# A hybrid decoder block: how far ahead the ada weights are fetched, how convolutions and SiLUs are spread over the half units, and the precision of the gate sums

## The chip, the core and the metric

One core of one Trainium2 chip runs the whole kernel. The metric is the device time of one execution in microseconds (us); the median of three runs of the kernel before is 1493.07 us (1491.11 to 1493.28).

## The reference

Only one layer and one sequence of 512 tokens are computed, with a model width of 2048.

```
shift, scale, gate = split(silu(c) @ w_ada + b_ada, 3)            # w_ada: 2048 x 6144
h = rms_norm(x) * (1 + scale) + shift                              # 512 x 2048
q_a k_a v_a z_a b_a a_a  q_b k_b v_b z_b  gl_a gl_b = h @ w_in     # w_in: 2048 x 10768
q,k,v = silu(causal_conv4(q_a k_a v_a)); q,k L2-normed
o_a = rms_norm(gated_delta_rule(q, k, v, g, beta)) * silu(z_a)     # 8 heads of 128
o_b = sliding_window_attention(q_b, k_b, v_b) * silu(z_b)          # 16 heads of 64
y = sigmoid(gl_a) * (o_a @ w_branch_gdn) + sigmoid(gl_b) * (o_b @ w_branch_swa)
out = x + gate * (y @ w_out)
```

## The kernel before

Every large product is done in fp32r with both factors split into a high and a low part: three matmuls of 128x128 by 512 stand for one in full precision. A weight **unit** is 512 KB of a weight matrix, loaded by one DMA on SyncE's queue (SP) into one of three `wraw` buffers (`w_dma`, L220); it serves two **half units**. For each half unit ScalarE (ACT) rounds its half of the unit to `whi` (L232), VectorE (DVE) subtracts to get `wlo` (L237), four buffers each, and TensorE (PE) does 12 matmuls. There are 464 half units; here they are H0 to H463, and the units U0, U1, ... (U19 serves H38 and H39, U20 serves H40 and H41).

`run(n)` (L242) writes the program one half unit at a time, in this order: the unit DMAs that are due (U(j+3) is due at H(2j+1)); the casts of the half unit two ahead (so H38's casts are written at H36); one step of each of the `lanes`; then the 12 matmuls. The schedule is by hand: every engine, and SP's queue too, executes its own instructions in the order in which the program wrote them, and waits at an instruction until its semaphores allow it. A tile's buffer is given to the next tile of its tag when all instructions that use the first tile are done, also those written later.

The first lane is `consumer` (L266). It empties three lists: all of `rel` (work that frees PSUM), one item of `hot`, and one item of `cons`. A convolution is two items (`conv_steps`, L409): `a` is a scaled copy and two taps on DVE, `b` is the third tap, a tanh on ACT, and a product on DVE that needs that tanh (L428). `silu2` (L432) is a tanh and such a product. The convolutions of the first group of heads go to `cons` (30 items, from H50), those of the second to `hot` (four items after every eight half units, from H72).

The second lane, `start_lane` (L1404), works out shift and scale while the matmuls already run. h is made in six stages (`STAGES`, 2, 2, 2, 2, 4 and 4 of the 16 column blocks of 128); the matmuls of one stage (`plan_start`) run while `ada_group(g)` prepares the next. Shift and scale of a stage are sums over 16 rows of blocks of `w_ada`: the first `DVEROWS[g]` rows on DVE (L348, L350), the rest on PE (L358, `ps_row`). Their weights come in 64 **pieces** of 512 KB, P0 to P63 (two DMAs each of 256 KB up to P31, L313; one from P32 on, L309), eight for each of the first four stages and sixteen for each of the last two. `ada_dma` sends them in order on SP's queue too; `send(r)`, after row r, sets how far they have been sent: `used` is the number of pieces used by then. Where a piece is put is in `HOMES`: a digit is one of the large buffers that later hold h, `s` a slot of a pool of 22. In the last stage (g = 5, P48 to P63, one row each, rows 0 to 11 on DVE) P60 and P61 have the buffer in which P52 and P53 (rows 4 and 5) were, and P62 and P63 that of P54 and P55 (rows 6 and 7). Its rows are prepared during H32 to H47: rows 0 and 1 at H32, 2 and 3 at H33, 4 and 5 at H35, 6 and 7 at H36. The `send` that reaches P61 is written after row 5, at H35, that which reaches P63 after row 7, at H36; U19 is due at H33, U20 at H35, U21 at H37.

Later lanes hold the delta rule (`gdn_all`, which starts when `cons` is empty), the keys, the attention, and `gate_all` (L1272): for each of four column blocks of 512 DVE sums 16 rows into `ga`, and one fp32 matmul with a matrix of ones adds the partitions (L1301).

Of the kernel before, what the change touches and what calls it, by code (L numbers as in the profile page):

```python
# [16 lines left out]
P = 128  # L17
# [20 lines left out]
def tile_hybrid_block(  # L38
# [32 lines left out]
    def s2(name, dt=F32):  # L71
        return sp.tile([P, 512], dt, tag="s2", name=nm(name), bufs=NS2)
# [7 lines left out]
    def side(name):  # L80
        return pq.tile([P, 512], F32, tag="side", name=nm(name))
# [103 lines left out]
    def split(hi, lo, src):  # L185
        S.copy(hi, src)
        V.tensor_tensor(lo, src, hi.bitcast(F32), op=ALU.subtract)
# [73 lines left out]
                after()  # L261
    run.s = 0

    cons, rel, hot = [], [], []

    def consumer():  # L266

        while True:
            while rel:
                rel.pop(0)()  # L270
            if hot:
                hot.pop(0)()
            if cons:
                cons.pop(0)()
            yield

# [54 lines left out]
    def ada_group(g):  # L331

        k0, nk = STAGES[g]
        nb = nk // 2
        first = [p_[0] for p_ in pieces].index(g)

        def send(r):

            used = first + r * nk // 4
            ada_dma(max(min(used + 12, 60), used + 8) - nada[0])  # L340

        nv = DVEROWS[g]
        av = None
        for r in range(nv):
            w = wada.pop((g, r))
            if r == 0:
                av = s4("accv")[:, 0:512 * nb]
                V.tensor_scalar(av, w, ccol[:, r:r + 1], None, op0=ALU.mult)  # L348
            else:
                V.scalar_tensor_tensor(av, w, ccol[:, r:r + 1], av, op0=ALU.mult, op1=ALU.add)  # L350
            if r % 2:
                send(r + 1)
                yield
        rows_ = [side("ps_row") for _ in range(nb)]
        for r0 in range(nv, 16, 4):
            for b_ in range(nb):
                for j in range(4):
                    TE.matmul(rows_[b_][32 * j:32 * j + 32], lhsT=cpad[:, r0 + j],  # L358
                              rhs=wada[g, r0 + j][:, b_ * 512:b_ * 512 + 512], start=(r0 == nv), stop=(r0 == 12))
            for r in range(r0, r0 + 4):  # L360
                del wada[g, r]
            send(r0 + 4)
            yield
        sums = s4("asum")[:, 0:512 * nb] if av is None else av
        for b_ in range(nb):
            bs = slice(b_ * 512, b_ * 512 + 512)
            if av is None:
                S.copy(sums[:, bs], rows_[b_])
            else:
                V.tensor_tensor(sums[:, bs], rows_[b_], av[:, bs], op=ALU.add)  # L370
        yield
        psum = small("psum", 8)
        for b_ in range(nb):
            ps = side("ps_mod")
            for i in range(4):
                TE.transpose(ps[:, i * P:(i + 1) * P], sums[:, (4 * b_ + i) * P:(4 * b_ + i + 1) * P], ident)
            if av is None:
                pv_ = ps.rearrange("p (i j z) -> p i j z", i=4, j=4)[:, :, :, 0]
            else:
                pv_ = v3(ps, 4)  # L380
            V.tensor_reduce(psum[:, 4 * b_:4 * b_ + 4], pv_, axis=AX.X, op=ALU.add)
        ks = slice(k0, k0 + nk)
        V.tensor_tensor(AB[:, :, ks], v3(psum[:, 0:2 * nk], 2),
                        cols[:, 0, 32:64].rearrange("p (w k) -> p w k", w=2)[:, :, ks], op=ALU.add)
        V.scalar_tensor_tensor(AB[:, 1, ks], AB[:, 1, ks], 1.0, gains[:, ks], op0=ALU.add, op1=ALU.mult)
        yield
        q, r0 = divmod(k0, 4)
        if r0 == 0:
            hhi[q] = hslot(q, 0, "hhi", F32R)
            hlo[q] = hslot(q, 1, "hlo", F32R)  # L390
        for i in range(nk):
            k, r = k0 + i, r0 + i
            a_, b_ = AB[:, 1, k:k + 1], AB[:, 0, k:k + 1]
            src = xnT[k // 2][:, k % 2]
            hf = s2("hf")
            S.activation(hhi[q][:, r], src, AF.Identity, scale=a_, bias=b_)
            if g < 2:
                V.tensor_scalar(hf, src, a_, b_, op0=ALU.mult, op1=ALU.add)
            else:
                S.activation(hf, src, AF.Identity, scale=a_, bias=b_)  # L400
            V.tensor_tensor(hlo[q][:, r], hf, hhi[q][:, r].bitcast(F32), op=ALU.subtract)
            if i % 2:
                yield


    def th_tile():
        return tp.tile([P, T], F32, tag="th", name=nm("th"), bufs=2)

    def conv_steps(o, src, ct):  # L409

        st = {}

        def tap(s):
            wcol = (3 - s) * 24 + ct
            V.scalar_tensor_tensor(st["o"][:, s:], src[:, :T - s], cw[:, wcol:wcol + 1], st["o"][:, s:],
                                   op0=ALU.mult, op1=ALU.add)

        def a():
            st["o"] = o()
            S.activation(st["o"], src, AF.Copy, scale=cw[:, 3 * 24 + ct:3 * 24 + ct + 1])  # L420
            tap(1)
            tap(2)

        def b():
            tap(3)
            th = th_tile()
            S.activation(th, st["o"], AF.Tanh, scale=0.5)
            V.scalar_tensor_tensor(st["o"], th, 1.0, st["o"], op0=ALU.add, op1=ALU.mult)  # L428

        return [a, b]  # L430

    def silu2(o, src):  # L432
        th = th_tile()
        S.activation(th, src, AF.Tanh, scale=0.5)
        V.scalar_tensor_tensor(o, th, 1.0, src, op0=ALU.add, op1=ALU.mult)

    zd = dp.tile([4, P, 1024], F32, name="zd")
    oad = dp.tile([8, P, 1024], F32, name="oad")
# [62 lines left out]
    def plan_tok(w, col, tile_of, consume, last=False):  # L501

        st = {}

        def mm(k):
            def f(hi, lo):
                if not st:
                    while hot:
                        hot.pop(0)()
                    st["ac"] = [acc("acct") for _ in range(NT)]  # L510
                st[k] = hi[:, 0], lo[:, 0]
                if last and k == KT - 2:
                    return
                for t in range(NT):
                    tsl = slice(t * P, (t + 1) * P)
                    for k_ in (k - 1, k) if last and k == KT - 1 else (k,):
                        wh, wl = st[k_]
                        sh, sl = (z[:, tsl] for z in tile_of(k_))
                        TE.matmul(st["ac"][t], lhsT=sh, rhs=wh, start=(k_ == 0), stop=False)  # L519
                        TE.matmul(st["ac"][t], lhsT=sh, rhs=wl, start=False, stop=False)  # L520
                        TE.matmul(st["ac"][t], lhsT=sl, rhs=wh, start=False, stop=(k_ == KT - 1))  # L521
                    if k == KT - 1:
                        consume(t, st["ac"][t])
            return f

        for ku in range(8):
            u = unit(w[ku * 256:(ku + 1) * 256, col:col + 512], 2)
            for hf in range(2):
                half(u, by_rows(2, hf), mm(2 * ku + hf))
# [62 lines left out]
    beta, hbeta, gg, eG, ekd, egl = (gv[:, i] for i in range(6))  # L592
    t0, t1, t2, t3 = (gv[:, 6 + i] for i in range(4))
    alr = kp.tile([P, P], F32R, name="alr")

    def hc(t):
        return t.rearrange("p (h c) -> p h c", h=GH)
# [3 lines left out]
    def gates_prep():  # L601


        nw = KT * 32
        wab = wab_.pop()
        wabr = s4("wabr", F32R)
        S.copy(wabr[:, nw:nw + 96], wab[:, KT * 16:KT * 16 + 96])
        wab3, wabr3 = v3(wab[:, 0:KT * 16], KT), v3(wabr[:, 0:nw], KT)
        S.copy(wabr3[:, :, 0:16], wab3)
        V.tensor_tensor(wabr3[:, :, 16:32], wab3, wabr3[:, :, 0:16].bitcast(F32), op=ALU.subtract)  # L610
        S.copy(alr, alow)
        S.activation(rows[:, 0:8], rows[:, 0:8], AF.Exp)
        wabs.append(wabr)

# [656 lines left out]
    def gate_all():  # L1271
        for ch in range(4):  # L1272
# [24 lines left out]
                yield  # L1297
            V.tensor_tensor(ga[0:1], ga[0:1], bg, op=ALU.add)
            yield
            pg = side("ps_gate")  # L1300
            TE.matmul(pg, lhsT=ones, rhs=ga, start=True, stop=True)  # L1301
            gates[ch] = s2("gb")
            S.activation(gates[ch], pg, AF.Copy, scale=0.5)
            yield
# [124 lines left out]

    def gdn_all():  # L1430
        yield from gdn_gates()
        while cons:
            yield
        yield from gdn_group(g0)
        while run.s < n_g1 + 5:
            yield
        yield from swa_bias()
        yield from gdn_group(g1)
        while run.s < n_swa + 2 or cons:
            yield  # L1440
        yield from swa_attend()
        yield from load_branches()
# [16 lines left out]
            if next(l_, l_) is l_:  # L1459
                lanes.remove(l_)  # L1460
    run(len(halves) - run.s)
    while rel or hot or cons:
        (rel or hot or cons).pop(0)()


_INS = ["x", "c", "w_ada", "b_ada", "norm_gain", "w_in", "conv_w", "a_log", "dt_bias", "gdn_norm_gain",
# [43 lines left out]
```

## Time and profile before

| | |
|---|---|
| median of 3 runs | 1493.07 us (1491.11 to 1493.28) |
| the profiled execution | 1491.63 us, span 1489.9 us |
| PE (matmul) busy | 1456.0 us, 98% |
| DVE, ACT, POOL busy | 846.3, 568.3, 63.8 us |
| granted PE clock over the span | 0.999 |
| DMA | 223.16 MB, mean 150 GB/s; 320 and 357 GB/s in the first two slices of 37.2 us |
| chain that ended last | PE 92%, DMA 3%, DVE 3%, ACT 1%, issue 1% |

A row of the timeline gives start and length in us, engine, line, operation, what it writes and reads, how many were merged, and in brackets the engine's idle time before it with what ended that. SPq is SP's queue: its rows are the issues of DMAs, and a merged row lasts from the first issue to the end of the last. Matmuls overlap: one takes some 390 ns, and the next starts 227 ns after it. Idle time of PE is therefore more than the bracket by the 0.16 us of overlap that is missing.

### The profile page before, as it was taken

What the parts mean: (1) busy time and instruction counts of PE and PEld (TensorE: products, weight loads), DVE (VectorE), ACT (ScalarE), POOL (GpSimd) and SP (SyncE); (2) the same over time, 40 slices, a digit from 0 to 9 for tenths busy, and PEclk for the clock granted to TensorE, in tenths of its full rate; (3) what the DMA queues carried; (4) which work ended last, traced back from release to release, by engine and by line L of the source; (5) the groups of instructions that cost most, each with busy time, mean ns of one, the idle gap of its engine ahead of it and who ended that gap; (6) DMA issues with size and microseconds to landing.
All of it is one profiled execution on the core that took longest, in us unless ns stands there. A gap on an engine that the chain in (4) does not pass through costs nothing.

```text
span 1489.9 us, 19141 instructions
## 1 busy us (share of the span) xinstructions
PE 1456.0 (98%) x7030; PEld 1190.8 (80%) x7030; DVE 846.3 (57%) x1724; ACT 568.3 (38%) x1275; POOL 63.8 (4%) x109
## 2 busy tenths in 40 slices
PE   4999999999999999999999999999999999999998
PEld 2676788788888888888888888888888888888887
DVE  4675977866755435643553578863324766664332
ACT  4424244363333453322442467763332322222221
POOL 0000000120200030200000000000000000000000
PEclk9999999999999999999999999999999999999999
DMA  9988433223522553422433332245547566564432
GB/s 320 357 277 285 146 101 100 84 86 85 156 63 66 170 171 102 143 82 85 134 93 99 102 97 86 86 135 178 169 127 253 193 225 234 183 207 147 156 125 87
DMA packets 163815, 223.16 MB, mean 150 GB/s; under 512 B 14741, under 2 KB 115414, under 8 KB 163722
## 3 DMA queue, kind: packets, MB, share of 16 engines
q1 hardware_dynamic: 155224, 207.87, 44.1%
q0 software_dynamic: 3616, 13.13, 2.6%
q10 hardware_dynamic: 4882, 0.94, 0.3%
q8 instruction: 55, 0.90, 0.2%
q14 instruction: 38, 0.31, 0.1%
HBM read 201.97 MB, written 23.09 MB: 151 GB/s over the span
## 4 chain that ended last, share of the span: by engine, by line
PE 92%; DMA 3%; DVE 3%; ACT 1%; issue 1%; SPq 0%; ACTq 0%
PE acc L190 17%; PE acc L192 17%; PE acc L191 17%; PE acct L520 7%; PE acct L519 7%; PE acct L521 7%; PE acc L553 3%; PE acc L554 3%; PE acc L559 3%; PE ps_row L358 1%; DMA wraw<-in_w_in_dram 1%; PE ps_kk L743 1%; PE ps_pT L1108 1%; PE ps_pv L1124 1%; DMA wada<-in_w_ada_dram 1%
## 5 line engine op out<-in xcount | busy, mean ns | idle before, releaser
L237 DVE TENSOR_TENSOR wlo<-wraw,whi 128x512 fp32r<-128x512 f32 x464 | 320.7, 693 | 446.4 <-ACT whi L232 439.8
L232 ACT CAST whi<-wraw 128x512 fp32r<-128x512 f32 x464 | 286.6, 621 | 585.7 <-PE acc L191 286.9
L190 PE MATMUL acc<-hhi,whi 128*128 128x512 f32 x896 | 356.3, 398 | 1.7 <-ACT whi L232 1.7
L192 PE MATMUL acc<-hhi,wlo 128*128 128x512 f32 x896 | 350.0, 391 | 0.7 <-DVE wlo L237 0.5
L191 PE MATMUL acc<-hlo,whi 128*128 128x512 f32 x896 | 349.2, 390 | 0.0
L192 PEld LDWEIGHTS acc<-hhi,wlo 128*128 128x128 f32 x896 | 168.2, 188 | 37.9 <-DVE wlo L237 1.9
L190 PEld LDWEIGHTS acc<-hhi,whi 128*128 128x128 f32 x896 | 168.4, 188 | 35.8 <-ACT whi L232 2.6
L191 PEld LDWEIGHTS acc<-hlo,whi 128*128 128x128 f32 x896 | 168.5, 188 | 33.0
L553 PE MATMUL acc<-hhi,whi 128*128 128x512 f32 x256 | 102.2, 399 | 4.5 <-ACT part L570 3.5
L190 PE MATMUL acc<-oh,whi 128*128 128x512 f32 x256 | 100.8, 394 | 0.0
L519 PE MATMUL acct<-whi,mh 128*128 128x512 f32 x256 | 100.1, 391 | 0.1
L554 PE MATMUL acc<-hhi,wlo 128*128 128x512 f32 x256 | 99.9, 390 | 0.0
L192 PE MATMUL acc<-oh,wlo 128*128 128x512 f32 x256 | 99.6, 389 | 0.0
L191 PE MATMUL acc<-ol,whi 128*128 128x512 f32 x256 | 99.6, 389 | 0.0
L520 PE MATMUL acct<-wlo,mh 128*128 128x512 f32 x256 | 99.6, 389 | 0.0
L521 PE MATMUL acct<-whi,ml 128*128 128x512 f32 x256 | 99.6, 389 | 0.0
L519 PE MATMUL acct<-whi,hhi 128*128 128x512 f32 x192 | 76.0, 396 | 0.0
L520 PE MATMUL acct<-wlo,hhi 128*128 128x512 f32 x192 | 74.9, 390 | 0.0
L521 PE MATMUL acct<-whi,hlo 128*128 128x512 f32 x192 | 74.8, 390 | 0.0
L559 PE MATMUL acc<-hlo,whi 128*128 128x512 f32 x256 | 68.5, 389 | 0.0
L553 PEld LDWEIGHTS acc<-hhi,whi 128*128 128x128 f32 x256 | 48.0, 188 | 25.6 <-issue 5.1
L572 DVE TENSOR_TENSOR part<-acc,part 128x512 f32<-128x512 f32 x80 | 51.4, 684 | 24.4 <-PE acc L559 24.4
(281 smaller groups left out, 1816.9 us busy)
## 6 DMA issues: line engine op xcount, KB each, us to landing
wraw<-in_w_in_dram SPq DMA_DIRECT2D x168, 512.0 KB, 3.7
wada<-in_w_ada_dram SPq DMA_DIRECT2D x64, 256.0 KB, 6.7
wada<-in_w_ada_dram SPq DMA_DIRECT2D x32, 512.0 KB, 6.3
wgate<-in_w_ada_dram SPq DMA_DIRECT2D x32, 512.0 KB, 5.7
wraw<-in_w_out_dram SPq DMA_DIRECT2D x32, 512.0 KB, 4.1
tgd<-tg SPq DMA_DIRECT2D x16, 512.0 KB, 2.9
wraw<-in_w_branch_gdn_dram SPq DMA_DIRECT2D x16, 512.0 KB, 3.4
wraw<-in_w_branch_swa_dram SPq DMA_DIRECT2D x16, 512.0 KB, 3.8
```

The costliest lines, as they stand in the source:

```text
L190: TE.matmul(o, lhsT=whi, rhs=mhi, start=start, stop=False)
L191: TE.matmul(o, lhsT=whi, rhs=mlo, start=False, stop=False)
L192: TE.matmul(o, lhsT=wlo, rhs=mhi, start=False, stop=stop)
L232: S.copy(casts[s][0], src)
L237: V.tensor_tensor(lo, view(raws[u]), hi.bitcast(F32), op=ALU.subtract)
L519: TE.matmul(st["ac"][t], lhsT=sh, rhs=wh, start=(k_ == 0), stop=False)
L520: TE.matmul(st["ac"][t], lhsT=sh, rhs=wl, start=False, stop=False)
L521: TE.matmul(st["ac"][t], lhsT=sl, rhs=wh, start=False, stop=(k_ == KT - 1))
L553: TE.matmul(st[ci][m], lhsT=hi[:, i, ms], rhs=mh_, start=(k == k0), stop=False)
L554: TE.matmul(st[ci][m], lhsT=lo[:, i, ms], rhs=mh_, start=False, stop=False)
L559: TE.matmul(st[ci][m], lhsT=hi[:, i, ms], rhs=ml_, start=False, stop=(k == k0 + nk - 1))
L572: V.tensor_tensor(part[ci][:, m], st[ci][m], part[ci][:, m], op=ALU.add)
```

## The change

Four things are changed. How far `send` goes ahead of `used`: it was 12 pieces, but no further than P59 until eight ahead is more than that; now it is 8 for the first two stages and wherever `used` is over 52, 10 for the third stage, 12 otherwise. The last product of a SiLU goes to a list `fin` that the consumer empties at the next half unit. The consumer takes an item of `cons` only if `hot` is empty. The sum `ga` is split into a high and a low part in fp32r, and two fp32r matmuls take the place of the fp32 one.

```diff
-    cons, rel, hot = [], [], []
+    cons, rel, hot, fin = [], [], [], []
     def consumer():
         while True:
             while rel:
                 rel.pop(0)()
+            while fin:
+                fin.pop(0)()
             if hot:
                 hot.pop(0)()
-            if cons:
+            elif cons:
                 cons.pop(0)()
             yield
...
         def send(r):
             used = first + r * nk // 4
-            ada_dma(max(min(used + 12, 60), used + 8) - nada[0])
+            ahead = 8 if g < 2 or used > 52 else 10 if g == 2 else 12
+            ada_dma(used + ahead - nada[0])
...
         def b():
             tap(3)
-            th = th_tile()
-            S.activation(th, st["o"], AF.Tanh, scale=0.5)
-            V.scalar_tensor_tensor(st["o"], th, 1.0, st["o"], op0=ALU.add, op1=ALU.mult)
+            silu2(st["o"], st["o"])
...
     def silu2(o, src):
         th = th_tile()
         S.activation(th, src, AF.Tanh, scale=0.5)
-        V.scalar_tensor_tensor(o, th, 1.0, src, op0=ALU.add, op1=ALU.mult)
+        fin.append(lambda: V.scalar_tensor_tensor(o, th, 1.0, src, op0=ALU.add, op1=ALU.mult))
...
                 if not st:
-                    while hot:
-                        hot.pop(0)()
+                    while fin or hot:
+                        (fin or hot).pop(0)()
...
+    onesr = kp.tile([P, P], F32R, name="onesr")
...
+        S.copy(onesr, ones)
...
+            gh_, gl_ = s2("gah", F32R), s2("gal", F32R)
+            split(gh_, gl_, ga)
+            yield
             pg = side("ps_gate")
-            TE.matmul(pg, lhsT=ones, rhs=ga, start=True, stop=True)
+            TE.matmul(pg, lhsT=onesr, rhs=gh_, start=True, stop=False)
+            TE.matmul(pg, lhsT=onesr, rhs=gl_, start=False, stop=True)
...
-        while cons:
+        while cons or fin:
             yield
...
-    while rel or hot or cons:
-        (rel or hot or cons).pop(0)()
+    while rel or fin or hot or cons:
+        (rel or fin or hot or cons).pop(0)()
```

## Rows read from the trace of the kernel before

**Rows 1.** The profile's busy part: engine, busy us, share of the span, instructions.
```profile
PE 1456.0 (98%) x7030; PEld 1190.8 (80%) x7030; DVE 846.3 (57%) x1724; ACT 568.3 (38%) x1275; POOL 63.8 (4%) x109
```

**Rows 2.** PE's list of waits: who waited for whom, us in total, times, longest.
```profile
PE ps_row L358 <- DMA wada<-in_w_ada_dram: 11.8, 1, 11.8
...
PE acc L553 <- ACT part L570: 3.5, 2, 1.9
PE ps_qT L1057 <- DVE qT L1062: 1.9, 3, 0.6
```

**Rows 3.** Timeline of SP's queue, 20 to 330 us.
```profile
40.50 7.71 SPq L313 DMA_DIRECT2D wada<-in_w_ada_dram  x10
48.63 0.37 SPq L224 DMA_DIRECT2D wraw<-in_w_in_dram  x1
```

**Rows 4.** Timeline of all engines, 46 to 75 us.
```profile
56.00 0.62 ACT L232 CAST whi<-wraw 128x512 fp32r<-128x512 f32 x1 [5.54 <-DMA wraw<-in_w_in_dram]
...
57.16 0.50 PE L553 MATMUL acc<-hhi,whi 128*128 128x512 f32 x1 [1.64 <-ACT part L570]
```

**Rows 5.** SP's own waits, 100 to 180 us; columns as in Rows 2.
```profile
SPq L309 <- DVE accv L350: 10.3, 2, 7.0
```

**Rows 6.** Timeline of SP's queue again, around stage 4.
```profile
132.42 22.41 SPq L224 DMA_DIRECT2D wraw<-in_w_in_dram  x5
161.89 5.79 SPq L309 DMA_DIRECT2D wada<-in_w_ada_dram  x4
167.77 10.93 SPq L224 DMA_DIRECT2D wraw<-in_w_in_dram  x4
```

**Rows 7.** Timeline of SP's queue, 120 to 128 us.
```profile
121.53 0.88 SPq L309 DMA_DIRECT2D wada<-in_w_ada_dram  x2
122.50 0.42 SPq L224 DMA_DIRECT2D wraw<-in_w_in_dram  x1
```

**Rows 8.** Line 224's only DMA of 120 to 131 us: issue to landing.
```profile
DMA to landing us min/median/max: 6.3/6.3/6.3
```

**Rows 9.** Timeline of DVE, 155 to 177 us.
```profile
159.26 2.60 DVE L350 SCALAR_TENSOR_TENSOR accv<-wada,cc,accv 128x1024 f32<-128x1024 f32 x2
161.78 0.69 DVE L237 TENSOR_TENSOR wlo<-wraw,whi 128x512 fp32r<-128x512 f32 x1
162.38 1.28 DVE L572 TENSOR_TENSOR part<-acc,part 128x512 f32<-128x512 f32 x2
163.58 2.60 DVE L350 SCALAR_TENSOR_TENSOR accv<-wada,cc,accv 128x1024 f32<-128x1024 f32 x2
166.10 1.29 DVE L237 TENSOR_TENSOR wlo<-wraw,whi 128x512 fp32r<-128x512 f32 x2
```

**Rows 10.** Timeline of ACT, 155 to 180 us.
```profile
175.16 1.14 ACT L232 CAST whi<-wraw 128x512 fp32r<-128x512 f32 x2 [8.33 <-DMA wraw<-in_w_in_dram]
```

**Rows 11.** Timeline of PE, 160 to 182 us: first matmuls, H38, H40.
```profile
166.01 0.39 PE L553 MATMUL acc<-hhi,whi 128*128 128x512 f32 x1
...
171.45 0.39 PE L553 MATMUL acc<-hhi,whi 128*128 128x512 f32 x1
```

**Rows 12.** Timeline of PE, 279 to 292 us.
```profile
281.59 0.50 PE L190 MATMUL acc<-hhi,whi 128*128 128x512 f32 x1 [0.31 <-ACT whi L232]
...
285.91 0.50 PE L192 MATMUL acc<-hhi,wlo 128*128 128x512 f32 x1 [0.48 <-DVE wlo L237]
...
289.91 0.50 PE L190 MATMUL acc<-hhi,whi 128*128 128x512 f32 x1 [1.40 <-ACT whi L232]
```

**Rows 13.** Timeline of PE, 1186 to 1189.5 us.
```profile
1186.92 1.02 PE L1301 MATMUL ps_gate<-ga,cs 128*128 128x512 f32 x2
...
1188.01 0.40 PE L191 MATMUL acc<-ol,whi 128*128 128x512 f32 x1
```

**Rows 14.** Stretches: each engine's busy us (count), PE clock, DMA share, GB/s.
```profile
1400.00:1487.00 87.00, 84.89 (x375) 69.96 (x373) 29.91 (x46) 17.26 (x28) 2.58 (x2) 1.00 0.42 136
1487.10:1490.00 2.90, 0.00 (x0) 0.00 (x0) 0.00 (x0) 0.00 (x0) 0.00 (x0) 0.50 0.24 90
```

## The prediction

> **What bounds the kernel now.** I read the busy part of the page first. PE is busy 98% of the span [rows 1], so a change can win only what PE still idles or does in a costlier way than it need, and it loses whatever it makes PE wait. Next comes PE's own list of waits [rows 2]: the largest, 11.8 us, is before the first shift-and-scale matmuls, where nothing of the change lies; then 3.5 us in the DMA-bound start. DVE, ACT and SP's queue have idle time, but PE keeps only the few half units of lead that the cast buffers give. So I went through the timeline half unit by half unit wherever the change moves an instruction, and asked each time whether something that PE needs now comes later than PE gets there.
>
> **The pieces, early stages (g below 3).** Ten DMAs, the five pieces P16 to P20, go out ahead of U3, which is issued only at 48.63 [rows 3]. Its cast on ACT starts at 56.00 after waiting for that load; copies that free a PSUM bank stand behind the cast, and PE stands 1.64 us for them [rows 4]. With eight ahead only P16 goes first, 8 DMAs fewer. These ten took 7.71 us to issue, so U3 leaves some 6 us sooner and that wait goes. What is late next: U4, behind two more pieces, which has a longer lead. I take 1.7 us won (0 to 1.7). The other half of the 3.5 us is U2, issued ahead of all this: no change. The pieces held back are used eight half units later, some 20 us, so DVE and PE don't miss them.
>
> **The pieces, last stage (g = 5).** Here the new rule does something else. After row 1, at H32, `used` is 50. Before, the limit was P59 until `used` passed 52; now 50 + 12 sends P60 and P61, and at H33, 52 + 12 sends P62 and P63. But P60 and P61 need the buffer of P52 and P53, which DVE reads as rows 4 and 5 at H35; P62 and P63 wait for rows 6 and 7 at H36. SP's queue keeps the written order, so it stands at P60 with everything behind it. That this wait is real shows before: SP waited twice, 10.3 us in all and 7.0 the longest, at line 309 for DVE's `accv` [rows 5], and P60 left at 161.89 [rows 6], just as rows 4 and 5 ended (159.26 + 2.60 [rows 9]). It cost nothing there, since the unit behind it was U21: it was issued at 167.77 [rows 6], held ACT 8.33 us, landed by 175.16 [rows 10], and is first needed at H42. U16 to U20 had left by 154.83 (132.42 + 22.41 [rows 6]). After the change U19, due at H33, stands behind P60 and P61, and U20 behind P62 and P63: each four half units nearer to its use.
>
> *How long such a unit takes* from the moment the two pieces are released: before, P62 and P63 were released when rows 6 and 7 ended (163.58 + 2.60 = 166.18 [rows 9]), and U21 behind them landed by 175.16: 9.0 us. Another pair with a unit behind it started at 121.53, and that unit, issued at 122.50 [rows 7], took 6.3 us [rows 8]: 7.3 us. So 7.3 to 9.0.
>
> *First block.* P60 leaves at 161.9, U19 lands at 169.2 to 170.9, the cast takes 0.6, and H38 starts at 169.8 to 171.5 instead of 166.01 [rows 11]: 3.8 to 5.5 us late. *Behind it on DVE* stand H38's `wlo`, two adds to `part`, and rows 6 and 7; from the start of that `wlo` to their end it was 161.78 to 166.18, 4.4 us [rows 9]. So P62 is released at 174.2 to 175.9, and H39's `wlo`, next on DVE, ends some 0.65 later, at 174.9 to 176.5. H39's second matmul needs it; PE does the other eleven in 2.5 us (24 matmuls took 171.45 − 166.01 = 5.44 us [rows 11], 227 ns each), until 177.4 to 179.0. *Second block.* U20 lands 7.3 to 9.0 us after the release, at 181.5 to 184.9, and with the cast H40 starts at 182.1 to 185.5 instead of 171.45: 10.7 to 14.1 us late, the first block's delay included. H40's own `wlo` adds 0.4 (0.69 less one matmul) and H42's about 0.2. After that U21 and the rest follow at once. PE has no idle time later in which to take this back. Cost 11.3 to 14.7 us; both measured cases are equally near, so I take 13.0. The lower end for the whole edit is 0, if the pieces were not to hold the queue.
>
> **One convolution to a half unit, and the late product.** At H72 to H75 `hot` and `cons` each give an item, so two convolutions fall on DVE in one half unit, and each `b` makes DVE wait for its tanh. PE's gaps there are 0.31, 0.48 and 1.40 us [rows 12]; each is 0.16 more against the 227 ns step, 2.7 us in all. One item to a half unit leaves DVE room, and the product finds its tanh done. I take 3.0, as gaps too short for a bracket go too (0 to 3.2). The price: of the 30 items of `cons` eight are left at H72; before they were gone at H79, now they alternate with `hot` and end at H87, the last product at H88, so the first delta-rule group starts nine half units later. Its instructions are the same and its successors have more lead than that; PE's waits for small tiles are at most 1.9 us in any one place before [rows 2], so I set it at 0 (0 to 2).
>
> **Gate sums.** The fp32 matmul and the one after it took from 1186.92 to 1188.01 [rows 13], 1.09 us; less one matmul of 0.227 it cost 0.87. Two fp32r matmuls cost 0.45. Four times 0.41 is 1.7 us (0 to 1.7). The four casts and subtractions go to ACT and DVE, 0.6 and 0.7 us each, half a unit ahead and with the gate not needed until the output; `onesr` is one copy.
>
> **The sum.** −1.7 − 3.0 − 1.7 + 13.0 = +6.6 us, on the profiled execution's 1491.63: 1498.2. That execution lies 1.4 below the median of the three runs; I put the forecast half way between, 1498.9, say 1499.0.
>
> **PE's clock.** It was granted at 1.00 (2.4 GHz) through everything up to 1487 us, short waits included, and at 0.50 (1.2 GHz) after PE had stopped [rows 14]. Whether it falls in the two new waits (3.8 to 5.5 us, then 4.7 to 6.5) no row tells: the longest wait inside the clocked stretch is under 2 us. If it does, a half unit of 2.72 us takes twice that: 2.7 us for one, 5.4 for both.
> The Trainium skill (TensorE: Matmul & The Clock Gate, "HAM oscillation — how this bites in real kernels") says that a matmul loop that waits long enough for DMA falls back to the slow clock and starts its next burst cold. By that rule the third rival below would be what happens.
>
> **The rivals.**
> *The queue's wait stays hidden*, because the buffer is handed over differently or the loads come faster: then only the gains remain, −6.4, 1486 us. For it: the same wait cost PE nothing before. Against: U19 and U20 have four half units less. Chance 0.12.
> *Only one block bites*: U20 lands in time, the loss is about 5 and the sum −1.4, 1491 to 1494 us. For it: the first landing can be as short as 7.3. Against: P62 can't leave before rows 6 and 7, which stand behind U19's cast. Chance 0.10, most of it within 0.2%.
> *The clock falls as well*: 1501.6 to 1504.3 us, decided by whether either wait is long enough. Chance 0.20.
> My forecast, both blocks at full clock, has 0.58, its own range 1497 to 1501.
>
> What a measurement of this kernel can tell from no change is 0.2%, 3 us. Faster: the first rival and a little of the second, 0.14; same 0.08; slower 0.78. The range of 1491 to 1504 leaves out the first rival and the edge of the third.
>
> **What would show it.** SP: line 309's last four issues in two pairs, each right behind DVE's rows 5 and 7, with U19 and U20 behind them; ACT waiting some 8 us or more for `wraw` twice between 150 and 185 us; PE idle some 4 and some 6 us there, and under 0.5 us at 57, at 280 to 290. Line 1301's matmuls 227 ns apart. Wrong would be: no idle time of PE over 2 us after the start (the first rival), or U20 ahead of P62 in SP's queue.

## The result, and the profile after

The changed kernel takes 1504.94 us (median of 4 runs, 1504.16 to 1505.62), the kernel before beside it 1493.17 us (1491.11 to 1495.27): a ratio of 1.0077, interval 1.0061 to 1.0093. It is slower, as forecast, but by 11.8 us and not by 6: the forecast was 1499.0, the range ended at 1504. The profiled execution took 1505.62 us, its span 1503.9, 14.0 more than before's.

The page's busy part, against [rows 1]: PE does as many matmuls, yet is busy 5.8 us longer. Longer matmuls, not only waits.

```profile
PE 1461.8 (97%) x7030; PEld 1196.1 (80%) x7030; DVE 848.3 (56%) x1728; ACT 570.4 (38%) x1280; POOL 63.7 (4%) x109
```

PE's list of waits (engine, line, waited for: us, times, longest), against [rows 2]; lines 555, 572 and 574 are before's 553, 570 and 572. Two waits of some 5 us are new, and a set of small ones at `ps_oT` and `ps_kT`, of which the prediction says nothing.

```profile
PE ps_row L361 <- DMA wada<-in_w_ada_dram: 10.7, 1, 10.7
...
PE acc L555 <- DVE part L574: 6.3, 3, 5.2
PE acc L555 <- ACT whi L232: 5.0, 1, 5.0
...
PE ps_oT L952 <- DVE kTl L1028: 1.5, 1, 1.5
PE ps_oT L952 <- DVE zs L953: 0.8, 1, 0.8
PE ps_kT L1021 <- DVE kvt L1008: 0.6, 1, 0.6
```

SP's own waits of 100 to 200 us, against [rows 5], then SP's queue, against [rows 6]. `accv` held the queue 32.9 us instead of 10.3. The pieces left in two pairs, P60 and P61 at 159.19, P62 and P63 at 171.66, with U19 and U20 behind them. Each wait began when the unit ahead had gone (130.13 + 7.10 = 137.23: 21.96 us of standing).

```profile
SPq L311 <- DVE accv L353: 32.9, 2, 21.9
```

```profile
130.13 7.10 SPq L224 DMA_DIRECT2D wraw<-in_w_in_dram  x3
159.19 0.88 SPq L311 DMA_DIRECT2D wada<-in_w_ada_dram  x2
160.18 0.41 SPq L224 DMA_DIRECT2D wraw<-in_w_in_dram  x1
171.66 0.88 SPq L311 DMA_DIRECT2D wada<-in_w_ada_dram  x2
172.64 13.08 SPq L224 DMA_DIRECT2D wraw<-in_w_in_dram  x4
```

ACT's casts there, then DVE, then PE's first matmuls of H38 and H40, against [rows 9 to 11].

```profile
166.58 1.14 ACT L232 CAST whi<-wraw 128x512 fp32r<-128x512 f32 x2 [13.31 <-DMA wraw<-in_w_in_dram]
179.67 1.14 ACT L232 CAST whi<-wraw 128x512 fp32r<-128x512 f32 x2 [11.95 <-DMA wraw<-in_w_in_dram]
```

```profile
156.57 2.60 DVE L353 SCALAR_TENSOR_TENSOR accv<-wada,cc,accv 128x1024 f32<-128x1024 f32 x2
167.23 0.69 DVE L237 TENSOR_TENSOR wlo<-wraw,whi 128x512 fp32r<-128x512 f32 x1 [8.06 <-ACT whi L232]
167.84 1.28 DVE L574 TENSOR_TENSOR part<-acc,part 128x512 f32<-128x512 f32 x2
169.04 2.60 DVE L353 SCALAR_TENSOR_TENSOR accv<-wada,cc,accv 128x1024 f32<-128x1024 f32 x2
...
180.93 1.28 DVE L574 TENSOR_TENSOR part<-acc,part 128x512 f32<-128x512 f32 x2
```

```profile
168.67 0.77 PE L555 MATMUL acc<-hhi,whi 128*128 128x512 f32 x1 [5.18 <-DVE part L574]
...
181.76 0.77 PE L555 MATMUL acc<-hhi,whi 128*128 128x512 f32 x1 [4.97 <-ACT whi L232]
```

The reader is to see the chain of one block: rows 4 and 5 end at 159.17, P60 goes at 159.19, U19 has landed by 166.58 (7.4 us), then cast, `wlo`, the first of two adds to `part`, and 0.83 us after that add began PE starts H38. Rows 6 and 7 end at 171.64, P62 goes at 171.66, U20 has landed by 179.67 (8.0 us), and again PE starts 0.83 us after the add began. The two waits are one pattern, though the list puts one down to `part` and the other to `whi`.

Both matmuls last 0.77 us where 0.39 was usual. The stretches (us, each engine's busy us and count, PE's clock, DMA share, GB/s) show why:

```profile
160.00:166.90 6.90, 3.49 (x16) 2.56 (x14) 0.00 (x0) 0.32 (x1) 0.00 (x0) 1.00 0.71 228
167.00:173.80 6.80, 5.13 (x12) 4.11 (x13) 4.97 (x6) 0.72 (x2) 0.00 (x0) 0.50 0.16 36
173.90:180.60 6.70, 2.89 (x13) 2.05 (x11) 0.28 (x1) 0.93 (x2) 0.00 (x0) 1.00 1.01 344
180.70:187.40 6.70, 5.64 (x16) 4.01 (x20) 6.63 (x8) 1.39 (x4) 0.00 (x0) 0.50 0.14 31
...
778.00:781.30 3.30, 3.30 (x9) 2.54 (x8) 1.88 (x3) 1.25 (x3) 0.00 (x0) 0.50 0.62 201
```

The clock was halved near the end of each wait, and H38 and H40 run at 1.2 GHz, a matmul each 427 ns. It is halved again at 778 us, after the small waits. By the Trainium skill (TensorE: Matmul & The Clock Gate, "HAM oscillation — how this bites in real kernels") a matmul loop that waits for DMA starts its next burst on the slow clock; for the two waits the trace agrees, 0.50 for 6.8 us each time.

**Where the 14.0 us are.** From the starts of PE's matmuls, twelve to a half unit, I took how much later each half unit starts than in the kernel before. The table gives how much that grows over a stretch, for each profiled execution (us); the run labels are those of the experiments below.

| | start, to H5 | H5–H31 | H31–H42 | H42–H64 | H64–H336 | to the end | span | ratio of the times (interval) |
|---|---|---|---|---|---|---|---|---|
| changed | −2.1 | −0.4 | +15.5 | +1.3 | +1.0 | −1.3 | +14.0 | 1.0077 (1.0061–1.0093) |
| e9, changed again | +0.7 | 0.0 | +14.3 | +1.3 | +1.0 | −1.3 | +16.0 | 1.0098 (1.0082–1.0113) |
| e10, PE filled | −2.0 | −0.4 | +13.2 | +1.3 | +0.8 | −1.3 | +11.7 | 1.0076 (1.0064–1.0089) |
| e3, PE filled | −1.0 | −0.4 | +13.3 | +1.3 | −0.6 | −1.3 | +11.4 | 1.0093 (1.0075–1.0110) |
| e2, one block | −1.7 | −0.4 | +7.2 | +1.3 | +1.0 | −1.3 | +6.1 | 1.0040 (1.0026–1.0054) |
| e1, old limit | −1.3 | +0.4 | 0.0 | +1.3 | +1.0 | −1.3 | +0.1 | 0.9995 (0.9986–1.0004) |
| e4, and keys later | +0.5 | −0.4 | −0.8 | +1.3 | −3.3 | −1.3 | −4.0 | 0.9969 (0.9959–0.9979) |
| e5, one convolution alone | +0.2 | +0.1 | 0.0 | 0.0 | +0.9 | −0.1 | +1.1 | 1.0004 (0.9994–1.0013) |
| e6, late product alone | +0.5 | −0.3 | 0.0 | +1.1 | +0.1 | 0.0 | +1.4 | 1.0009 (1.0000–1.0019) |
| e7, pieces and gates alone | −1.5 | −0.3 | 0.0 | 0.0 | 0.0 | −1.3 | −3.1 | 0.9994 (0.9985–1.0004) |
| e8, e4 with gate casts early | −1.5 | 0.0 | +0.4 | +0.3 | −3.2 | −1.3 | −5.4 | 0.9966 (0.9953–0.9979) |

The first column holds up to 3 us that change from one execution of a kernel to the next (the changed kernel's two profiles: −2.1 and +0.7). The other columns of those two agree within 0.4, but for H31 to H42, 15.5 and 14.3, on which more at e10.

### The profile page after: what moved, and what is told of

Its sections match the earlier page's. It is cut to its first block, busy times and chain, and to the rows that moved or that the text cites. A ratio compares the mean times of both kernels' runs of the same rounds, so it can differ in the third digit from the quotient of the medians.

```text
span 1503.9 us, 19151 instructions
## 1 busy us (share of the span) xinstructions
PE 1461.8 (97%) x7030; PEld 1196.1 (80%) x7030; DVE 848.3 (56%) x1728; ACT 570.4 (38%) x1280; POOL 63.7 (4%) x109
## 4 chain that ended last, share of the span: by engine, by line
PE 89%; DVE 5%; DMA 3%; ACT 2%; issue 1%; SPq 0%; ACTq 0%
PE acc L190 17%; PE acc L192 17%; PE acc L191 17%; PE acct L521 6%; PE acct L522 6%; PE acct L523 6%; PE acc L555 3%; PE acc L556 3%; PE acc L561 3%; DMA wraw<-in_w_in_dram 1%; PE ps_row L361 1%; PE ps_kk L747 1%; PE ps_pT L1112 1%; PE ps_pv L1128 1%; DVE kq L418 1%
## 5 line engine op out<-in xcount | busy, mean ns | idle before, releaser
L555 PE MATMUL acc<-hhi,whi 128*128 128x512 f32 x256 | 104.5, 408 | 13.3 <-DVE part L574 6.3
```

Source lines behind the costliest of these rows:

```text
L555: TE.matmul(st[ci][m], lhsT=hi[:, i, ms], rhs=mh_, start=(k == k0), stop=False)
```

## The experiments

**e1: the changed kernel with the old limit.** Theory: both blocks come from sending P60 to P63 before their buffers are free. Rival: the DMA traffic of the pieces makes U19 and U20 late.

```diff
-            ada_dma(used + ahead - nada[0])
+            ada_dma(max(min(used + ahead, 60), used + 8) - nada[0])
```

> The changed kernel with the old limit put back in the last stage alone: no piece past P59 until eight ahead is more. Theory (SP's queue stands at P60 and P62 with U19 and U20 behind them, PE waits for those, and its clock falls in the waits): everything that PE lost from H32 to H41, 15.7 us in the two profiles, goes; no clock of 0.50 between 150 and 200 us; the span is 1503.9 - 15.7 = about 1488, the time about 1489 to 1490. Rival (the loss is DMA traffic that the other distances of the earlier stages pushed into this stretch): the early distances stay, so a gap of PE of 2 us or more stays between 150 and 190 us and the time stays above 1497.

Measured: 1490.77 us (1489.14 to 1493.72, 10 runs) beside 1491.17. H31 to H42 are as before, and PE is busy through the whole stretch:

```profile
160.00:190.00 30.00, 30.00 (x145) 23.52 (x144) 25.01 (x37) 9.15 (x15) 0.00 (x0) 1.00 0.62 183
```

The four pieces alone make the loss; the rival falls. But 1490.77 is above the 1486 that the other gains promised: something else costs some 5 us.

**e2: only the first block.** With `used > 50`, P62 and P63 go out when they went before.

```diff
-            ahead = 8 if g < 2 or used > 52 else 10 if g == 2 else 12
+            ahead = 8 if g < 2 or used > 50 else 10 if g == 2 else 12
```

> The changed kernel with eight ahead from used over 50 instead of over 52, so P60 and P61 are still sent at H32, but P62 and P63 only at H36 as before the change. Theory: the first wait stays as it is (5.3 us of PE before H38, and H38 at the low clock), H39 still waits for its wlo behind rows 6 and 7, but U20 is issued right behind U19 and the second wait of 5.1 us before H40 is gone, with the second fall of the clock (2.7 us): 7.5 to 8 us faster than the changed kernel, about 1497. Rival (the second wait is a late effect of the first, as DVE and ACT run behind, and not P62 in the queue): a wait of 3 us or more before H40 stays, about 1503.

Measured: 1497.69 us (1496.73 to 1497.87, 5 runs). P62 left at 172.37, but now with U20 ahead of it (two units at 160.70), and the second wait is gone. SP's queue and PE's one wait:

```profile
159.72 0.88 SPq L311 DMA_DIRECT2D wada<-in_w_ada_dram  x2
160.70 0.96 SPq L224 DMA_DIRECT2D wraw<-in_w_in_dram  x2
172.37 0.88 SPq L311 DMA_DIRECT2D wada<-in_w_ada_dram  x2
```

```profile
169.37 0.76 PE L555 MATMUL acc<-hhi,whi 128*128 128x512 f32 x1 [5.38 <-ACT whi L232]
```

Each pair is a block of its own: the first alone costs 7.2 us with its slow half unit, and the second adds 8.3 (15.5 − 7.2).

**e3 and e10: PE kept busy in the waits.** Is the clock's fall a cost of its own? Twenty matmuls that nothing reads stand ahead of H38 and of H40.

```diff
+    def fill():
+        pf = side("ps_fill")
+        for _ in range(20):
+            TE.matmul(pf, lhsT=hhi[0][:, 0, 0:P], rhs=hhi[0][:, 0], start=True, stop=True)
+    before(38, fill)
+    before(40, fill)
```

> The changed kernel with 20 matmuls of 128x128 by 512 more before H38 and before H40, on data that is there and into a PSUM bank that nobody reads: some 4.5 us of work in each of the two waits of 5.3 and 5.1 us. Theory (PE's clock falls because it idles there): with PE at work the granted clock stays at 1.00 through 160 to 190 us, H40 takes 2.7 us instead of some 5.2 and H38 2.7 instead of 5.2 up to its wait for wlo, and although 40 matmuls are added the kernel is 2 to 4 us faster than the changed one, 1501 to 1503. Rival (the half units after the waits are slow because their operands still arrive late): no gain, or up to 1 us slower, 1505 to 1506.

Measured: 1504.94 us (1502.98 to 1508.17, 4 runs). The profile did what the theory said, clock 1.00 throughout and H31 to H42 13.3 us later, not 15.5. The times did not: the median is the changed kernel's own, and the ratio to the kernel before, 1.0093, lies above its 1.0077. The two had not been timed side by side, so I ran them together on one chip.

> The changed kernel itself once more, so that the next kernel can be set against it in the same session. In its first profile the time came out 11.8 us over the kernel before by the medians, 14.0 by the profiled spans. Expected here: 11 to 14 us over the kernel before, granted clock 0.50 after both new waits of H38 and H39/H40.

> The changed kernel with 20 matmuls of PE that nothing reads ahead of H38 and of H40, so that PE does something in the new waits. Theory (the fall of PE's clock after the waits costs 2.4 to 2.7 us): granted clock 1.00 through both, and the time 2 to 4 us under the changed kernel beside it. Rival (the slow clock hides under what is late anyway, or the added matmuls cost as much as they save): within 1 us of it.

Measured: the changed kernel 1506.92 us (1505.68 to 1508.56, 4 runs), 14.7 over the kernel before beside it (1492.21) and so above the 11 to 14 expected; filled 1504.11 (1501.79 to 1504.48, 5 runs): 2.8 us less, and no run of the one reaches the other's. The filled kernel's PE, and the stretch at H38:

```profile
163.35 4.69 PE L1373 MATMUL ps_fill<-hhi 128*128 128x512 f32 x20
169.67 0.47 PE L555 MATMUL acc<-hhi,whi 128*128 128x512 f32 x1 [1.62 <-DVE part L574]
...
175.96 4.70 PE L1373 MATMUL ps_fill<-hhi 128*128 128x512 f32 x20
182.19 0.47 PE L555 MATMUL acc<-hhi,whi 128*128 128x512 f32 x1 [1.54 <-DVE part L574]
```

```profile
167.00:173.80 6.80, 4.76 (x20) 3.37 (x19) 4.97 (x6) 1.14 (x2) 0.00 (x0) 1.00 0.03 3
```

By the profiles the filled kernel loses less from H31 to H42 than the changed one, by 2.2 us against its first profile and 1.0 against its second. The two differ because the loads do: from the moment a pair left to the cast of the unit behind it, it took 7.4 and 8.0 us in the changed kernel's first profile, 6.9 and 7.2 in its second, 8.4 and 7.4 in e10, 8.8 and 7.6 in e3. With the two landings of each taken off, H31 to H42 stands at 0.1 and 0.2 in the changed kernel and at −2.6 and −3.1 in the filled ones. So I estimate the fall at some 2.7 to 3.2 us. The times say 2.8 for the two kernels run together and nothing for the changed kernel's first runs and e3, taken apart; they hold the start's changes too.

It is not the 5.4 of two slow half units: in the changed kernel H40 starts 12.8 us later than before against H31, in e10 13.1. The 2.5 us that the slow H38 loses vanish in the second block, whose end DVE and the DMA set; only H40's 2.7 us remain.

**e4: where the other 5 us are.** With the old limit PE's largest new waits are at 750 to 770 us (764 to 782 in the changed kernel). There the last steps of the second delta-rule group, nine half units later than before, lie beside the keys' lane, which starts at a fixed half unit. In the kernel before, PE had done that group's transposes into `ps_oT` (in H207 and H208) some 19 us ahead of the keys' (into `ps_kT`, in H215 and H216):

```profile
737.62 1.03 PE L948 MATMUL ps_oT<-cs,kv 128*128 128x128 f32 x8
...
757.55 0.60 PE L1017 MATMUL ps_kT<-cs,kvt 128*128 128x128 f32 x4
```

In the changed kernel's profile they fall in H216 and H217, among the keys (PE, then DVE, then ACT):

```profile
767.25 0.33 PE L1021 MATMUL ps_kT<-cs,kvt 128*128 128x128 f32 x1 [0.60 <-DVE kvt L1008]
...
775.90 0.63 PE L952 MATMUL ps_oT<-cs,kv 128*128 128x128 f32 x4 [1.48 <-DVE kTl L1028]
777.31 0.66 PE L952 MATMUL ps_oT<-cs,kv 128*128 128x128 f32 x4 [0.79 <-DVE zs L953]
```

```profile
772.38 0.68 DVE L1028 TENSOR_TENSOR kTl<-ps_kT,kTh 64x512 fp32r<-64x512 f32 x1 [0.65 <-ACT kTh L1027]
...
776.51 1.41 DVE L953 SCALAR_TENSOR_TENSOR zs<-ps_oT,ghalf,zs 128x512 f32<-128x512 f32 x2
```

```profile
773.10 0.58 ACT L1027 CAST kTh<-ps_kT 64x512 fp32r<-64x512 f32 x1 [0.75 <-DVE kTl L1028]
```

The keys go from `ps_kT` in four pairs of an ACT cast and a DVE subtraction, each waiting for the other, some 1.34 us a pair (772.38 to 773.72). The group's `zs` product, which frees a bank that PE's transposes into `ps_oT` want, stands behind them on DVE, and PE behind that. The keys started twelve half units later should undo it.

```diff
-        while run.s < n_gla + 18 or cons:
+        while run.s < n_gla + 30 or cons:
```

> As e1_cap, and the lane that prepares the keys starts twelve half units later, at H222 instead of H210, after the second delta-rule group has ended (H219 now, H210 before the change). Theory (the nine half units by which the delta rule starts later put its last transposes beside the keys, and PE waits there 1.6, 0.95 and 0.8 us and then runs at the low clock for 1.6 us more): these 4.9 us go, so 4 to 5 us faster than e1_cap, about 1485, with no clock of 0.50 near 760 us. Rival (the delta rule's tail is slow by itself beside the token-wise products of the swa stage): the waits before ps_oT stay and the time is that of e1_cap within 1 us.

Measured: 1486.89 us (1486.11 to 1489.62, 9 runs), 3.9 us under e1 beside it. PE has no idle time left there, at full clock:

```profile
760.00:790.00 30.00, 30.00 (x138) 24.81 (x137) 19.04 (x44) 13.99 (x26) 0.00 (x0) 1.00 0.35 108
```

H64 to H336 went from +1.0 (e1) to −3.3: the collision cost 4.2 us, 1.6 of them its own stretch of slow clock (a `ps_oT` wait followed by 778 to 781 at 0.50; in e3, where PE has the same waits and the clock didn't fall, the stretch stands at −0.6 instead of +1.0).

```profile
760.00:785.00 25.00, 22.13 (x108) 17.89 (x107) 19.21 (x43) 10.63 (x22) 0.00 (x0) 1.00 0.29 93
```

**e5 and e6: which edit brings it.** One convolution to a half unit alone, on the kernel before, and the late product alone. (e6 is the change's hunks with `fin`, and no more.)

```diff
-            if cons:
+            elif cons:
                 cons.pop(0)()
```

> The kernel before with one edit: an item of cons only where hot is empty. Theory: the crowd of DVE at H72 to H79 goes (about 3 us won) and the late delta rule collides with the keys (about 4 us lost, with waits before ps_oT near 765 us): from H64 to H221 between 0 and +2 us against before, nothing at H48 to H64, time within 2 us of before. Rival (the collision comes from the late product and not from the order of the lists): no wait before ps_oT, H64 to H221 about -3 us, time 3 us less than before.

Measured: 1492.14 us (1490.85 to 1493.22, 10 runs) beside 1491.61. PE's gaps of [rows 12] are all gone, as they are in the changed kernel, and the win is given back near 768 us. The wait there was expected before `ps_oT`; it stands before a `whi` instead, whose cast ACT does right behind the last of the keys' casts (the group moved by eight half units here, not nine):

```profile
768.81 0.79 PE L519 MATMUL acct<-whi,hhi 128*128 128x512 f32 x1 [2.42 <-ACT whi L232]
```

> The kernel before with one edit: the last product of a SiLU goes to the next half unit, ahead of that half unit's own item. Theory: the product stands on DVE ahead of the next convolution's taps, its tanh on ACT stands ahead of the casts for the gates and of whi, and PE waits near H61 to H64: about +1.3 us from H48 to H64, as in the changed kernel. At H72 to H79 two convolutions still fall in one half unit but DVE no longer waits 0.76 us for each tanh: 0.5 to 2.5 us won there; no collision with the keys. Time within 1.5 us of before. Rival (the wait at H62 comes from the one copy that the gates' edit adds to ACT): nothing at H48 to H64.

Measured: 1492.59 us (1491.56 to 1494.01, 10 runs), an interval from 1.0000. The late product loses 1.1 us at H62, about as expected. The win expected at H72 to H79 fails: where [rows 12] have gaps of 0.31, 0.48 and 1.40, this kernel has one of 1.67 and two small ones (0.23, 0.57), and H64 to H336 stands at +0.1. Two convolutions in a half unit still fill DVE, and now it is `wlo` that comes late:

```profile
287.56 0.50 PE L192 MATMUL acc<-hhi,wlo 128*128 128x512 f32 x1 [1.67 <-DVE wlo L237]
```

The win is the one convolution's, and so is the collision.

The place at H62, in the changed kernel:

```profile
243.80 0.74 DVE L418 SCALAR_TENSOR_TENSOR kq<-part,cols,kq 128x509 f32<-128x509 f32 x1
244.63 0.63 ACT L436 ACTIVATE th<-kq 128x512 f32<-128x512 f32 x1 [4.19 <-DVE kq L418]
245.17 0.26 ACT L610 CAST wabr<-wab 128x96 fp32r<-128x96 f32 x1
...
246.15 0.60 ACT L232 CAST whi<-wraw 128x512 fp32r<-128x512 f32 x1
...
247.40 1.28 DVE L574 TENSOR_TENSOR part<-acc,part 128x512 f32<-128x512 f32 x2
248.23 0.47 PE L555 MATMUL acc<-hhi,whi 128*128 128x512 f32 x1 [0.79 <-DVE part L574]
```

The last half unit's product now stands ahead of the taps on DVE; so the third tap and, behind it on ACT, the tanh, the casts of the gates' weights and H64's `whi` come later, and so do DVE's adds, for whose bank PE waits.

**e7: early pieces and gates alone**, on the kernel before and with the old limit for P60 to P63.

> The kernel before with the pieces 8, 10 and 12 ahead but the old limit in the last stage, and the gate sums in fp32r; the lists are as before. Theory: -1.7 us from H3 to H5 and -1.3 to -1.8 us from H336 to the end, nothing between: 3.0 to 3.5 us less than before. Rival (what the early half units win is given back before H38, since DMA is busy there and the pieces only come later): -1.7 us at the end alone.

Measured: by the profile −3.1 us, as expected, with −1.72 at H3 to H5 and −1.30 after H336. By the times 1490.83 (1488.58 to 1493.86, 10 runs) beside 1491.61, an interval that holds 1: not resolved. One cause shows. The start's wait for U2, which all these kernels have, sometimes is followed by half the clock at 48 to 52 us; in the two profiles with early pieces in which it did (e4, e9), H3 to H5 won 0.11 instead of the 1.70 to 1.72 of the seven others.

**e8: a kernel that keeps the gains.** e4 with the gates' casts taken from H60 to H48, away from the convolutions.

```diff
-    run(n_start - 4 - LATE)
+    run(n_start - 16 - LATE)
     gates_prep()
-    run(4)
+    run(16)
```

> As e4_cap_keys, and the casts for the gates are written at H48 instead of H60, before the first convolution. Theory (the wait near H62 is ACT's queue: a tanh that waits for DVE, then 1.3 us of casts, then whi): the +1.3 us from H48 to H64 go, so 1 to 1.5 us faster than e4_cap_keys, about 1485.5, 5.5 us less than before. Rival (DVE itself is too full there): a wait of PE of 0.5 us or more stays between H60 and H64 and the time is that of e4_cap_keys.

Measured: 1486.22 us (1485.72 to 1487.95, 5 runs) beside 1491.61, a ratio of 0.9966 (0.9953 to 0.9979): it beats both kernels. By the profile H42 to H64 lost 0.3 instead of 1.3; against e4 by the times the 0.7 us lie within what the two measurements leave open.

## Why the prediction was wrong

*The early pieces*: right. −1.7 was forecast and −1.72 measured. U3 left at 41.61 instead of 48.63 [rows 3]; measured from U2's issue (38.65, before 39.92) that is 5.7 us sooner, where I had said some 6.

```profile
41.61 0.37 SPq L224 DMA_DIRECT2D wraw<-in_w_in_dram  x1
```

*The two blocks*: right, in mechanism and size. The pairs left right behind DVE's rows; the landings took 7.4 and 8.0 us of the 7.3 to 9.0 allowed; at full clock both cost 13.2 (e10) against 13.0. One detail was missing: after the cast PE waits not for `whi` but for `wlo` and the first add to `part` behind it, 2.1 us from cast to matmul, not the 0.6 that I allowed. Landings at the short end made up for it.

*PE's clock*: the rival with chance 0.20 was what happened. I gave it the smaller chance because the trace had no wait between 2 us and a full stop. Its price was half right: some 2.7 to 3.2 by the estimate at e10, about one half unit, and I said 2.7 to 5.4.

*One convolution and the late product*: the win was right, −3.3 (e4) against −3.0. **The step that failed is "its successors have more lead than that ... so I set it at 0 (0 to 2)"** for the first delta-rule group nine half units later. Its successor had no such lead. The second group starts when the first is done (PE did its first transposes in H144, behind the first's last in H142, and now does them in H153, behind H151), so it moved by the same nine half units, and its end met a neighbour that did not move: the keys, which start at a half unit counted from elsewhere, at H215 and H216 in both kernels. That cost 4.2 us. I had given no row for the successor's lead, and not asked what runs beside the moved work in its new place.

*The late product's price* was left out of the sum: +1.1 to 1.3 at H62, on DVE's and ACT's order.

*The gates*: 1.3 against 1.7. The two matmuls now stand 0.23 us apart [rows 13], four times 0.45 won, 0.3 lost at one place near 1325 us, 0.2 spread.

```profile
1204.94 0.39 PE L1308 MATMUL ps_gate<-gah,onesr 128*128 128x512 f32 x1
1205.17 0.39 PE L1309 MATMUL ps_gate<-gal,onesr 128*128 128x512 f32 x1
```

The miss by the spans is 7.4 us (14.0 − 6.6): 4.2 for the collision, 2.3 for the clock (the changed kernel's first profile against e10), 1.3 for H62, 0.4 for the gates and 0.2 for the blocks, less 0.4 more than forecast in the start, 0.4 in H5 to H31 and 0.3 more from the convolutions: 7.3. Against the median it is 5.9, since the forecast stood 0.8 above the sum and the changed kernel's profiled execution 0.7 above its median. No case of mine held two mishaps: the third rival's 1501.6 with the collision's 4.2 is 1505.8, beyond the range's 1504.

Two things stay open: why the changed kernel's first runs and e3, taken apart, show no gain from the filling in their times where the profiles do, and why the clock stayed at 1.00 near 778 us in e3, behind the very waits after which it fell in the other kernels. I didn't test either.

## What to carry to other kernels

A prefetch limit that looks like "further ahead is safer" has to be read against the buffers: a DMA issued before its buffer is free holds its queue, and the price is paid by the next, unrelated load behind it. When work is moved, list not only what waits for it but what already runs on its engines at the new place; lanes that start at fixed points don't move along. And a wait of PE like the two here, of some 5 us, should be priced twice, once for the time and once for the half unit after it at half clock, less what the next wait hides.

## What the runs showed of the hardware

The clock fell after waits much shorter than I had thought of: after 1.48 and 0.79 us, with four transposes between, it was 0.50 for 3.4 us at 778; in e3 the same two waits, as long and with the same transposes, left it at 1.00. After the start's wait for U2 it was 0.50 near 48 to 52 us where the wait had been 2.03, 2.09 and 3.31 us (e4, e5, e9), and stayed at 1.00 where it had been 2.19 and 2.27 (e8, e3): the length of the wait alone doesn't decide it. Twenty matmuls into a bank that nobody reads, 4.7 us long, held it at 1.00 through both waits, although PE still stood 1.5 to 2.0 us after them.
